# Two transformer blocks on one core: new prices in the clock that orders side work among weight products

## The chip, the cores and the metric

One core of a Trainium2 chip runs the whole program. The metric is the device time of one execution in microseconds; before the change the median of three runs is 2108.08 us (2105.86 to 2108.32).

## What is computed

The reference applies two layers of a first block and then two layers of a second block to a sequence of 256 tokens of width 1024, all in float32. A layer of the first block is a mixer (a gated linear recurrence, a forgetting attention of 8 heads with a cumulative decay, and a retention of 4 heads), a cross attention of 4 heads against a memory of 256 tokens, and a gated feed-forward of width 2816. A layer of the second block is a feed-forward, a mixer, and a feed-forward. Its mixer has a compressed, a selected and a window attention whose results are added under gates, a stick-breaking attention, and a window attention with sink logits:

```python
y_nsa = nsa_attention(...); y_sb = stick_breaking_attention(...); y_swa = swa_sink_attention(...)
merged = (g[:, :, 0] * (y_nsa @ w_up_nsa[l]) + g[:, :, 1] * (y_sb @ w_up_sb[l])
          + g[:, :, 2] * (y_swa @ w_up_swa[l]))
x = x + merged @ w_out[l]
```

## The kernel before

**Weight products.** All weights are read once, in pieces of 1 MB (raw). ScalarE rounds a piece to a high part (whi), VectorE subtracts to get the low part (wlo), and TensorE multiplies in three passes (high x high, high x low, low x high) in the dtype F32R. The activations, transposed, are held as thi and tlo; an output collects in a PSUM tile acc. A weight product of 512 columns is the unit of the main work. Weights.take and Weights.done (lines 235 to 265) hand out a piece and then start the splitting of the next. Callers are nat_blocks, stat_block, out_rows, fill_steps and, in the second mixer, up (line 1829).

**Side work.** What lies between the weight products (attention scores, softmax, transposes, normalisations) is written as generators. side(gen) (line 328) adds one to a list; pump() (line 336) advances those that are due. nat_blocks pumps after each half piece, which is six weight products of 512 columns; up pumps only in its second half. A generator yields the time at which its next step may come: True stands for the end of what it has just issued, None for at once, False for a flag to be waited for. Small products and transposes write to two PSUM banks called aux; two_aux() (line 370) waits until both are free. pairs() (line 375) is the pipeline of an attention over pairs of heads: scores, then row sums (rows), then transposes (turned), then value products (out), with waits between them. fox() (line 943) and nsa() (line 1665) use it, as do swa() and sb().

**The clock.** Nothing is measured while the program runs. The order is fixed when it is built, by the class Pace (line 49). It carries an estimated time for each engine, and nc.products is the time that TensorE has reached. Each call of an engine moves its time by a price: a fixed part and a part for each element (FIXED), a rate for TensorE, 360 GB/s and 1.5 us for a DMA. A step counts as due when its time is at most nc.products + 0.3, the advance. need(T, kt, t) (line 450) is asked before each weight product; if the k tile isn't made yet it pumps with force, which issues the earliest step whatever its time and moves nc.products there.

**What needs what.** In the first mixer the output products take k tiles 2 to 5 first; these are the forgetting attention's, which ends with value products into M. In the second mixer up(0, 4, 4, False) (line 1856) takes Y's k tiles 0 to 3, which nsa() writes in two groups of four units; a unit is one pair of heads in one branch, and the last group is tiles 2 and 3. Engines work through their own instructions in program order, so a step issued too early holds up what stands behind it on its engine.

Of the kernel before, what the change touches and what calls it, by code (L numbers as in the profile page):

```python
# [9 lines left out]
F32R = mybir.dt.float32r  # L10
# [38 lines left out]
class Pace:  # L49

    FIXED = {"vector": (0.065, 1.045e-3), "scalar": (0.075, 0.86e-3), "gpsimd": (0.13, 2.15e-3)}

    TABLES = {AF.Exp: ("exp", "ln"), AF.Tanh: ("exp",), AF.Ln: ("ln",), AF.Sin: ("sin",), AF.Sqrt: ("sqrt",), AF.Silu: ("silu",)}

    def __init__(self, nc):
        self.nc, self.table = nc, None
        self.products = self.end = 0.0
        self.at, self.written, self.read, self.free = {}, {}, {}, {}  # L60
        self.loads = 0.0
        for name in ("tensor", "vector", "scalar", "gpsimd", "sync"):
            self.at[name] = 0.0
            setattr(self, name, Paced(self, name, getattr(nc, name)))
# [22 lines left out]
    def op(self, name, op, args, kwargs):  # L87
# [15 lines left out]
        elif name == "tensor":  # L103
            moving = aps[2] if op == "matmul" else aps[0]
            rate = 1 if moving.dtype == F32R else 2 if op == "transpose" else 4
            self.products = start + max(0.027, size(moving) * rate / 2400.0) + 0.004
            done = self.products + 0.1
        else:
            fixed, each = self.FIXED[name]
            n = max(size(a) for a in aps)  # L110
            if kwargs.get("op") == ALU.pow:
                fixed, each = 0.3, 0.165
            if name == "scalar" and op == "activation":
                f = next((a for a in list(args) + list(kwargs.values()) if isinstance(a, AF)), None)
                if f in self.TABLES and self.table not in self.TABLES[f]:
                    self.table = self.TABLES[f][0]
                    self.at[name] = max(start, self.at[name]) + 1.3
            self.at[name] = max(start, self.at[name]) + (fixed + each * n) + (0.09 if kwargs.get("accum_out") is not None else 0.0)
            done = self.at[name] + 0.1
        for a in [out, kwargs.get("accum_out")]:  # L120
# [148 lines left out]
def tile_two_blocks(ctx, tc, I, out):  # L269
# [51 lines left out]

    def mm(ps, a, b, start, stop):
        nc.tensor.matmul(ps, a, b, start=start, stop=stop)

    def turn(ps, src, by):
# [10 lines left out]
    def pump(force=False):  # L336
# [15 lines left out]
        for _ in range(len(sides) + 1):  # L352
            ready = [i for i in sides if not i[2]]
            due = [i for i in ready if i[1] <= nc.products + 0.3 and aux_free() <= nc.products + 0.3]
            if due:
# [14 lines left out]
    def two_aux():  # L370

        while max([nc.idle(a) for a in auxs[-2:]], default=0.0) > nc.products + 0.3:
            yield max(nc.idle(a) for a in auxs[-2:])
# [30 lines left out]
    def pair_scores(q, k):  # L404

        pss = aux(), aux()
        for c, qs, ks in ((slice(0, P), slice(0, P), slice(0, P)), (slice(P, 384), slice(P, S), slice(0, S))):
            for u in (0, 1):
                mm(pss[u][:, c], q[HALF[u], qs], k[HALF[u], ks], start=True, stop=True)
        return pss  # L410

    def pair_scores_T(q, k):

        pss = aux(), aux()
        for c, ks, qs in ((slice(0, S), slice(0, P), slice(0, S)), (slice(S, 384), slice(P, S), slice(P, S))):
            for u in (0, 1):
                mm(pss[u][:, c], k[HALF[u], ks], q[HALF[u], qs], start=True, stop=True)
        return pss
# [19 lines left out]
    def pair_pv(dst, ws, vs, start=True, stop=True):  # L438

        for kt, (c0, c1, q0) in enumerate(((0, S, 0), (S, 384, P))):  # L440
            for u in (0, 1):
                mm(dst[HALF[u], q0:S], vs[u][:, kt, :], ws[u][:, c0:c1], start=start and kt == 0, stop=stop and kt == 1)

# [442 lines left out]
    def mixer1(l, T, cos, sin, next_maker):  # L886
        with nc.pool(tc, name=nm("mix1"), bufs=2) as mp:
# [26 lines left out]
            def forget(a):  # L914
# [24 lines left out]
                nc.vector.tensor_copy(c, ps[:8, :S])  # L939
                nc.sync.dma_start(cdram, c)  # L940


            def fox():
# [33 lines left out]
                def out_(b):  # L977
# [4 lines left out]
                    if b % 2 == 1:  # L982
                        put_T(M, 1 + b, ob[0])

                load_nb(0)
                load_nb(1)
# [1050 lines left out]
```

## Time and profile before

| | us |
|---|---|
| median of three runs | 2108.08 |
| the profiled execution | 2107.61 |
| its span, first to last instruction | 2105.8 |
| TensorE products busy | 2053.1 |
| VectorE busy | 1276.0 |
| ScalarE busy | 1120.7 |
| GpSimd busy | 84.7 |

The mean granted clock of TensorE is 0.995 of full speed. A line of the profile is always L150 in this kernel, because all calls pass through one helper there; instructions are told apart by their tiles (out<-in, buffer numbers left out). acc is a weight product; aux and o are side products. The end of a product is modelled and overlaps the next, so the distance between starts tells its cost better than its length. An fp32 product of the side work shows as two instructions, a transpose and an F32R product as one.

### The profile page before, as it was taken

To read this page: it belongs to the slowest core of one execution; us is meant where nothing else is said; L and a number is where in the kernel's file an instruction comes from. 1 tells how busy PE (TensorE), PEld (TensorE's weight loads), DVE (VectorE), ACT (ScalarE), POOL (GpSimd) and SP (SyncE) were. 2 spreads that over 40 slices of the span, in tenths; PEclk is the share of its full clock that TensorE was granted. 3 is DMA by queue.
4 is the path that set the end of the run, shared out by engine and by line. 5 is a ranking of instruction groups with operands and counts; after the bars stand their busy time and mean duration, and the time that the engine had idled before them with its cause. 6 is when DMAs were issued, how large, how long until landed. Compare 5 with 4: busy or idle time off the path is not lost.

```text
span 2105.8 us, 28507 instructions
## 1 busy us (share of the span) xinstructions
PE 2053.1 (97%) x10982; PEld 1717.3 (82%) x10982; DVE 1276.0 (61%) x2187; ACT 1120.7 (53%) x1910; POOL 84.7 (4%) x110
## 2 busy tenths in 40 slices
PE   7999999999899999999999999999999999999999
PEld 6889888888797788788888767888888887768887
DVE  6766566556664755655467666664655567756553
ACT  5556566455465654555355655554555456446552
POOL 0210000002100000000001000000000001000000
PEclk9999999999999999999999999999999999999999
DMA  7555565654465565555646544555555547545553
GB/s 244 182 194 190 186 212 180 212 178 158 148 225 175 182 198 191 172 187 180 210 145 207 169 140 158 193 176 193 180 196 194 162 151 230 144 132 183 179 197 103
DMA packets 204583, 380.86 MB, mean 181 GB/s; under 512 B 14160, under 2 KB 78464, under 8 KB 204448
## 3 DMA queue, kind: packets, MB, share of 16 engines
q1 hardware_dynamic: 192928, 366.46, 53.1%
q10 hardware_dynamic: 11520, 12.59, 2.0%
q8 instruction: 86, 1.41, 0.3%
q14 instruction: 49, 0.40, 0.1%
HBM read 372.03 MB, written 6.99 MB: 180 GB/s over the span
## 4 chain that ended last, share of the span: by engine, by line
PE 83%; DVE 6%; ACT 4%; DMA 4%; issue 2%; POOL 0%; SPq 0%; ACTq 0%; DVEq 0%; POOLq 0%
PE acc L150 74%; PE aux L150 6%; DVE wlo L150 3%; PE o L150 3%; ACT whi L150 1%; DMA nb<-cdram 1%; DMA raw<-in_w_in_dram 1%; DMA w<-in_nsa_cmp_k_w_dram 1%; ACT rn L150 1%; ACT thi L150 1%; DMA kvd<-kvout 0%; SPq L150 0%; DVE t L150 0%; DVE h L150 0%; DMA mem<-in_mem_dram 0%
## 5 line engine op out<-in xcount | busy, mean ns | idle before, releaser
L150 PE MATMUL acc<-whi,thi 128*128 128x512 f32 (+2 forms) x1856 | 716.2, 386 | 2.3 <-ACT thi L150 1.4
L150 PE MATMUL acc<-whi,tlo 128*128 128x512 f32 (+2 forms) x1856 | 699.9, 377 | 2.5 <-DVE tlo L150 2.4
L150 PE MATMUL acc<-wlo,thi 128*128 128x512 f32 (+2 forms) x1856 | 699.3, 377 | 3.1 <-DVE wlo L150 2.8
L150 DVE TENSOR_TENSOR wlo<-raw,whi 128x1024 fp32r<-128x1024 f32 (+1 forms) x386 | 463.0, 1210 | 310.1 <-ACT whi L150 308.3
L150 ACT CAST whi<-raw 128x1024 fp32r<-128x1024 f32 (+1 forms) x386 | 393.7, 1037 | 243.9 <-PE acc L150 219.9
L150 DVE SCALAR_TENSOR_TENSOR wlo<-raw,prm,whi 128x512 fp32r<-128x512 f32 (+1 forms) x640 | 398.5, 680 | 173.8 <-ACT whi L150 173.6
L150 ACT ACTIVATE whi<-raw,prm 128x512 fp32r<-128x512 f32 (+1 forms) x640 | 379.9, 663 | 90.2 <-PE acc L150 86.7
L150 PEld LDWEIGHTS acc<-whi,thi 128*128 128x128 f32 x1856 | 350.3, 189 | 72.4 <-issue 9.3
L150 PEld LDWEIGHTS acc<-whi,tlo 128*128 128x128 f32 x1856 | 349.9, 189 | 70.3 <-DVE tlo L150 6.4
L150 PEld LDWEIGHTS acc<-wlo,thi 128*128 128x128 f32 x1856 | 350.5, 189 | 64.4 <-DVE wlo L150 6.1
L150 PE MATMUL acc<-whi,ahi 128*128 128x512 f32 x528 | 206.9, 392 | 0.0
L150 PE MATMUL acc<-whi,alo 128*128 128x512 f32 x528 | 205.7, 389 | 0.0
L150 PE MATMUL acc<-wlo,ahi 128*128 128x512 f32 x528 | 205.6, 389 | 0.0
L150 PEld LDWEIGHTS acc<-whi,alo 128*128 128x128 f32 x528 | 99.1, 188 | 20.8
L150 PEld LDWEIGHTS acc<-whi,ahi 128*128 128x128 f32 x528 | 99.2, 188 | 19.9
L150 PEld LDWEIGHTS acc<-wlo,ahi 128*128 128x128 f32 x528 | 99.2, 188 | 19.9
L150 POOL TENSOR_TENSOR r<-v,mhalf 128x1 f32<-128x1 f32 (+3 forms) x46 | 48.1, 1047 | 1593.9 <-DVE v L150 1591.9
L150 PE MATMUL acc<-thi,whi 128*128 128x256 f32 x384 | 111.9, 291 | 0.0
L150 PE MATMUL acc<-tlo,whi 128*128 128x256 f32 x384 | 108.6, 283 | 0.0
L150 PE MATMUL acc<-thi,wlo 128*128 128x256 f32 x384 | 108.5, 283 | 0.0
L150 DVE SCALAR_TENSOR_TENSOR silu<-acc,r,silu 128x512 f32<-128x512 f32 (+1 forms) x72 | 47.5, 702 | 100.4 <-PE acc L150 100.4
L150 ACT CAST ahi<-aux 128x512 fp32r<-128x512 f32 (+1 forms) x72 | 39.8, 553 | 121.9 <-PE aux L150 121.7
(301 smaller groups left out, 1946.9 us busy)
## 6 DMA issues: line engine op xcount, KB each, us to landing
raw<-in_w_in_dram SPq DMA_DIRECT2D x65, 1024.0 KB, 5.1
raw<-in_ffn_w_gate_dram SPq DMA_DIRECT2D x44, 1024.0 KB, 5.1
raw<-in_ffn_w_up_dram SPq DMA_DIRECT2D x44, 1024.0 KB, 5.1
raw<-in_ffn_w_down_dram SPq DMA_DIRECT2D x44, 1024.0 KB, 4.9
raw<-in_w_gate_dram SPq DMA_DIRECT2D x22, 1024.0 KB, 5.0
raw<-in_w_up_dram SPq DMA_DIRECT2D x22, 1024.0 KB, 5.1
raw<-in_w_down_dram SPq DMA_DIRECT2D x22, 1024.0 KB, 4.8
raw<-in_w_out_dram SPq DMA_DIRECT2D x16, 1024.0 KB, 5.0
```

Source lines behind the costliest of these rows:

```text
L150: return f(*args, **kwargs)
```

## The change

Pace gets other prices. VectorE, ScalarE and GpSimd have larger fixed parts; activations have a price of their own; a sum that an activation collects costs 0.19 us more instead of 0.09; results count as ready 0.15 us after an engine's end (0.1 before) and 0.25 us after TensorE's (0.1 before). A transpose costs 0.109 us; the second product of a pair that runs on the other half of the array (beside) 0.007 us, where before it cost as much as the first; a weight product its columns and 32 more at 2.4 GHz; going from weight products to side products or back 0.09 us. The advance of 0.3 us is taken out of pump() and two_aux(). The prices of DMAs stay. In the first mixer forget() now sets a flag when it has issued the write of cdram, and fox() waits for that flag before its first loads. The arithmetic is the same in all steps.

```diff
-    FIXED = {"vector": (0.065, 1.045e-3), "scalar": (0.075, 0.86e-3), "gpsimd": (0.13, 2.15e-3)}
+    FIXED = {"vector": (0.15, 1.06e-3), "scalar": (0.14, 0.89e-3), "gpsimd": (0.25, 3.3e-3)}
...
-            rate = 1 if moving.dtype == F32R else 2 if op == "transpose" else 4
-            self.products = start + max(0.027, size(moving) * rate / 2400.0) + 0.004
-            done = self.products + 0.1
+            main = moving.dtype == F32R
+            if op == "transpose":
+                took = 0.109
+            elif self.beside:
+                took = 0.007
+            elif main:
+                took = (size(moving) + 32) / 2400.0
+            else:
+                took = max(0.224, size(moving) * 4 / 2400.0)
+            self.products = start + took + (0.09 if main != self.main else 0.0)
+            self.main = main
+            done = self.products + 0.25
...
-                fixed, each = 0.3, 0.165
+                fixed, each = 0.5, 0.22
...
-            self.at[name] = max(start, self.at[name]) + (fixed + each * n) + (0.09 if kwargs.get("accum_out") is not None else 0.0)
-            done = self.at[name] + 0.1
+            if name == "scalar" and op == "activation":
+                fixed, each = 0.3, 0.8e-3
+            self.at[name] = max(start, self.at[name]) + (fixed + each * n) + (0.19 if kwargs.get("accum_out") is not None else 0.0)
+            done = self.at[name] + 0.15
...
-    def mm(ps, a, b, start, stop):
+    def mm(ps, a, b, start, stop, beside=False):
+
+        nc.beside = beside
         nc.tensor.matmul(ps, a, b, start=start, stop=stop)
+        nc.beside = False
...
-            due = [i for i in ready if i[1] <= nc.products + 0.3 and aux_free() <= nc.products + 0.3]
+            due = [i for i in ready if i[1] <= nc.products and aux_free() <= nc.products]
...
-        while max([nc.idle(a) for a in auxs[-2:]], default=0.0) > nc.products + 0.3:
+        while max([nc.idle(a) for a in auxs[-2:]], default=0.0) > nc.products:
...
-                mm(pss[u][:, c], q[HALF[u], qs], k[HALF[u], ks], start=True, stop=True)
+                mm(pss[u][:, c], q[HALF[u], qs], k[HALF[u], ks], True, True, beside=u > 0)
...
                 nc.sync.dma_start(cdram, c)
+                flags.add("cdram")
...
+                while "cdram" not in flags:
+                    yield False
                 load_nb(0)
```

The same beside=u > 0 stands in pair_scores_T and pair_pv.

## Rows read from the trace of the kernel before

**Rows 1.** The page's table of engines: busy us, share of span, instructions.
```profile
PE 2053.1 (97%) x10982; PEld 1717.3 (82%) x10982; DVE 1276.0 (61%) x2187; ACT 1120.7 (53%) x1910; POOL 84.7 (4%) x110
```

**Rows 2.** Chain that ended last, a feed-forward stage: start us, length us, what.
```profile
328.31 20.45 PE acc L150 x90
```

**Rows 3.** Busy us by engine in a second mixer and a feed-forward; then clock, DMA.
```profile
1070.00:1280.00 210.00, 202.19 (x1156) 160.20 (x1156) 138.77 (x299) 115.09 (x218) 10.48 (x6) 0.99 0.54 166
...
1492.00:1682.00 190.00, 188.95 (x908) 158.02 (x907) 109.56 (x152) 97.34 (x149) 1.24 (x3) 1.00 0.56 187
```

**Rows 4.** TensorE's waits in the whole span: total us, times, longest us.
```profile
PE aux L150 <- DVE rn L150: 6.0, 4, 2.1
PE aux L150 <- DMA w<-in_nsa_cmp_k_w_dram: 3.8, 2, 2.6
PE aux L150 <- DVE rs L150: 2.9, 2, 1.5
...
PE aux L150 <- ACT cqT L150: 2.4, 2, 1.2
...
PE o L150 <- DVE rvg L150: 2.2, 1, 2.2
PE aux L150 <- DVE sc L150: 2.0, 1, 2.0
PE aux L150 <- DVE fT L150: 1.9, 1, 1.9
...
PE aux L150 <- DVE rot L150: 1.7, 2, 1.5
...
PE aux L150 <- ACT pt L150: 1.1, 1, 1.1
```

**Rows 5.** Chosen stretches, as rows 3 (the third last column is granted clock).
```profile
77.40:80.80 3.40, 3.40 (x11) 2.58 (x11) 3.29 (x8) 0.96 (x2) 0.00 (x0) 0.50 0.39 115
538.20:545.00 6.80, 6.61 (x30) 6.10 (x31) 3.50 (x10) 2.48 (x3) 0.87 (x2) 0.50 0.23 87
...
1253.90:1266.80 12.90, 9.09 (x49) 5.32 (x48) 5.03 (x21) 4.37 (x14) 0.00 (x0) 0.87 0.00 1
...
1869.60:1881.00 11.40, 7.87 (x49) 4.46 (x48) 5.00 (x21) 4.02 (x13) 0.00 (x0) 1.00 0.00 1
```

**Rows 6.** Timeline, short windows: start us, length us, engine, operation, [idle before, releaser].
```profile
1216.64 0.82 PE L150 MATMUL aux<-ident,rn 128*128 128x128 f32 x6
1217.21 0.49 PE L150 MATMUL acc<-whi,thi 128*128 128x512 f32 x1
1217.54 0.40 PE L150 MATMUL acc<-wlo,thi 128*128 128x512 f32 x1
...
1218.47 0.40 PE L150 MATMUL acc<-whi,tlo 128*128 128x512 f32 x1
1218.79 0.93 PE L150 MATMUL aux<-kT,qT 64*128 64x128 f32 x8
1219.65 0.50 PE L150 MATMUL acc<-whi,thi 128*128 128x512 f32 x1
...
1248.80 0.93 PE L150 MATMUL aux<-kT,qT 64*128 64x128 f32 x8
...
1250.15 0.40 ACT L150 ACTIVATE rn<-rn,nngm 128x128 f32<-128x128 f32 x1 [2.10 <-DVE nngm L150]
...
1251.83 0.18 ACT L150 ACTIVATION_READ_ACCUMULATOR rn<-rn,nngm 128x1 f32 x1
...
1255.79 1.16 PE L150 MATMUL aux<-ident,rn 128*128 128x128 f32 x6 [0.98 <-DVE rn L150]
...
1261.35 1.44 PE L150 MATMUL aux<-ident,rn 128*128 128x128 f32 x6 [2.06 <-DVE rn L150]
...
148.60 0.87 PE L150 MATMUL o<-pt,fv 128*64 128x256 f32 x8
149.40 0.50 PE L150 MATMUL acc<-whi,thi 128*128 128x512 f32 x1
```

More of the change, by code (lines that the diff above doesn't have):

```diff
@@ L61, in __init__ @@
         self.loads = 0.0
+        self.beside = False
+        self.main = True
         for name in ("tensor", "vector", "scalar", "gpsimd", "sync"):
@@ L416, in pair_scores_T @@
             for u in (0, 1):
-                mm(pss[u][:, c], k[HALF[u], ks], q[HALF[u], qs], start=True, stop=True)
+                mm(pss[u][:, c], k[HALF[u], ks], q[HALF[u], qs], True, True, beside=u > 0)
         return pss
@@ L441, in pair_pv @@
             for u in (0, 1):
-                mm(dst[HALF[u], q0:S], vs[u][:, kt, :], ws[u][:, c0:c1], start=start and kt == 0, stop=stop and kt == 1)
+                mm(dst[HALF[u], q0:S], vs[u][:, kt, :], ws[u][:, c0:c1], start and kt == 0, stop and kt == 1, beside=u > 0)
     def put_T(T, kt0, ob):
```

## The prediction

> **What bounds the kernel now.** I read the page's engine table first. TensorE multiplies for 97% of the span, VectorE works for 61% and ScalarE for 53% [rows 1]. The chain of waits shows what that busy time is. In its long pieces 90 weight products of 512 columns take 20.45 us, 0.227 us each, with nothing between them [rows 2]. Where only weight products run, the planner can win nothing. The table by stage shows where it is otherwise: in a second mixer TensorE is without work for 7.8 us of 210, in a feed-forward stage for 1.0 of 190 [rows 3]. The list of TensorE's waits names what it waits for. The start aside, it is tiles of side work of the mixers and the cross attention: rn, rs, cqT, rvg, sc, fT, rot, pt, and a small weight load by DMA [rows 4]. The table of chosen stretches adds the granted clock: 0.50, that is 1.2 GHz for 2.4, in two stretches of the first mixer, each during or right after such waits [rows 5].
>
> So two things can move. One is steps issued before their input is ready: TensorE, which works in program order, stands. The other is steps issued later than they could be: the chain of a mixer then isn't done when its result is needed, and TensorE stands at the end. The second is seen in both layers of the second mixer. There the weight products want Y's third k tile, the window and selection attention has not delivered it, and the planner forces what is left: 12.9 us in the first layer, 11.4 us in the second, with almost no weight product in it [rows 5].
>
> **The change part by part.** It changes no computation; it prices the same calls differently, so that pump() issues them at other places. The work on TensorE stays: only waits, visits and clock move. (A visit to side work costs about 0.19 us: the last weight product before one is followed after 0.32 us and the first after one after 0.33 us, where 0.23 is the rule [rows 6].)
>
> *Steps too early.* The old prices let the step after a pair of score products come 1.82 us after them: 0.10 for TensorE, 0.199 + 0.10 for the first VectorE pass, 1.32 for four exponentials with sums, 0.10 to finish; the advance takes 0.30 off, so 1.52 us. The trace has 2.35 us, from the end of the products at 1249.66 (1248.80 plus the 0.86 that the same group takes at 1218.79) to the last accumulator read at 1252.01 [rows 6]. So such a step is issued 0.8 us early, unless the grid of pump calls (six weight products, 1.36 us) rounds it up. That is the origin of waits on rs (2.9 us), cqT (2.4), sc (2.0) and fT (1.9), 9.2 us in all [rows 4]. New prices cover each: I count 8.0 us gone, bounds 3 and 9.2.
>
> *Waits that the new prices don't see.* rvg (2.2 us): the step asks for a flag that is set when the copy is issued, and no time is asked for, before or after. rot (1.7): VectorE stands for a DMA of decay rows, and the DMA lines are unchanged. pt (1.1): ScalarE stands behind an output copy. These 5.0 us go only where the steps land elsewhere: I count 2.0 us gone, bounds 0 and 5.0. The wait on the compression weights (3.8 us) is a DMA too: 0, bounds 0 and 3.8.
>
> *Clock.* The stretch 77.4 to 80.8 follows the wait on sc: 3.4 us at half rate cost 1.7. The one at 538.2 to 545.0 lies in the rvg and rot waits and costs up to 3.4 [rows 5]. I count the first and a third of the second: 2.8 us gone, bounds 0 and 5.1.
>
> *Steps later than needed.* A unit of the selection and window attention has three waits. Scores to row sums: 1.52 us before; now 0.25 + 0.286 + 0.15 + 2.57 + 0.15 = 3.41 us. Row sums to transposes: two small operations and four scalings, 1.30 - 0.30 before, 1.87 now; the value products between them used to push the planner's clock by 1.30 us and now do by 0.85, so 0.45 more is to be waited. Transposes to the next scores: 1.01 - 0.30 before, 1.36 now. Together 1.89 + 0.87 + 0.45 + 0.65 = 3.86 us more for each unit. In the trace three units take 30.0 us, from the scores at 1218.79 to those at 1248.80 (first and last of four) [rows 6]: 10.0 each, of which 2.8 us is TensorE's own (0.86 scores, 0.80 values, 0.57 transposes, three visits at 0.19; the 0.80 is that of the same eight products in the other mixer at 148.60) and the rest 5.3 grid steps. With the new waits rounded up to the grid, 3 to 4 + 1 to 2 + 1 to 2, it is 5 to 8 steps, 6.5 in the middle. So each unit is later by 2.0 us (by the rounding) to 3.9 us (by the sum). Three units: 6 to 12 us. The four units before them share their two banks with other chains whose prices rise as well; their delay can't be read from a row, and I put it between 2 and 12 us. At 12 to 14 us a unit the chain arrives at the forced place 0.6 to 2 units short; I take 1.5.
>
> What is a unit worth there? In the forced stretch two successive transposes stand at 1255.79 and 1261.35, 5.56 us apart [rows 6]. Of this, 2.8 us would have been paid earlier anyway. So a unit pushed into the tail costs 2.76 us: 1.5 x 2.76 x 2 layers = 8.3 us added, bounds 0 and 16.6 (three units).
>
> Here a rule of the Trainium skill speaks against the change. The four exponentials follow one another at 1250.15 and end with the last read at 1252.01: 1.86 us, so a read of 0.18 us overlaps the next exponential [rows 6]. The page "ScalarE: Activation LUTs" (Rules for kernel authors) has about 0.3 us for an ACTIVATE plus 0.83 ns an element; that is an estimate of 1.84 us for these four, and the trace agrees. By that rule the change's 2.57, which adds 0.19 for each sum, is 0.7 us too long, and the rows step would be held back by half a grid step without need.
>
> *The first mixer's end.* Its forgetting attention ends with the value products at 148.60; the output products start behind them at 149.40 [rows 6], and need this tile only in their third piece, two pieces of 12 products or 5.4 us later. The same added wait over four units is 8 to 15 us, so one step may be forced there. It would stand for little, since in the trace its inputs are ready long before: 1.0 us added over both layers, bounds 0 and 6. The new flag for cdram holds fox() until the row sums are written; with a flag already set it costs nothing, else one pump.
>
> *New places, new waits.* Every side step of the mixers may land on a busier moment of VectorE or ScalarE. I add 1.0 us, bounds -2 and 5. The feed-forward stages have few side steps and no wait to lose: 0.
>
> **The sum**, against the profiled execution's 2107.6 us (span 2105.8 and 1.8 around it): - 8.0 - 2.0 - 2.8 + 8.3 + 1.0 + 1.0 = - 2.5, so 2105.1. The median of the runs shown is 2108.1, 0.5 above that execution, so 2105.6; I say 2105.5.
>
> **The rivals.** *Gains without the loss.* The rounding eats the longer prices, the tails stay, and all early steps are cured: - 9.2 - 3 - 4 and nothing added, about 2092, and 2102 if only the sure part goes. For it: in the four units of the trace the steps already wait for the grid. Against it: 3.86 us is nearly three grid steps, too much to be rounded away three times in a row.
>
> *The tail takes over: slower.* One mechanism, in one place: the forced stretch before Y's third k tile in both layers of the second mixer. At three units late it costs 16.6 us, and with half of the savings (6.4) and the other additions (2.0) the time is 2108.1 + 16.6 - 6.4 + 2.0 = 2120; with 2.3 units 2116. It decides from where added tail exceeds the savings: 12.8 - 2.0 = 10.8 us, or about 2 units a layer. For it: 3.86 us a unit over eight units is 31 us, over two periods. Against it: five to six units lie in stretches where other chains hold them back already. The clock joins in: in the first layer's tail it was 0.87 on average, in the second's 1.00, with like gaps in the work [rows 5], so it can fall there but need not. The page "TensorE: Matmul & The Clock Gate" (What's actually happening) holds that idleness brings the engine to half rate; by that rule longer tails would run at 1.2 GHz in both layers and add, estimated from the 3.4 us stretch of these rows, up to 1.7 us each.
>
> *It does little.* The grid decides most steps, the order hardly changes, and the waits named above are DMA and queue waits that no engine price cures: 2106 to 2111.
>
> **How the numbers follow.** Chances: forecast (losses and gains nearly balance, 2100 to 2111) 0.38; gains without loss (2092 to 2102) 0.28; tail takes over (2111 to 2121) 0.25; little 0.09. About 0.2%, 4.2 us, is what a measurement of this kernel can tell from no change. Faster by more, below 2103.9: 0.13 of the forecast's and all 0.28 of the first rival, 0.41. Slower by more, above 2112.3: 0.23 of the tail's, 0.03 of the forecast's, 0.01 of the last: 0.27. The rest is 0.32. Cases of both signs hold most of the chance, so the range over all is 2094 to 2118 beside the forecast's own 2100 to 2111.
>
> **What would show it.** In the profile after: the waits on cqT, sc, fT and rs shrink to under 3 us together, while rvg, rot and the compression weights may stay. Full clock at 77 to 81 us. In the second mixer fewer units before the forced stretch: score products further apart than 10.0 us, and a stretch of 15 to 22 us in place of 12.9. I am wrong if that stretch is no longer than before, if the waits on these four tiles persist, or if the feed-forward stages change.

## The result, and the profile after

The changed kernel takes 2164.98 us, median of four runs (2162.41 to 2166.85), against 2108.2 us for the kernel before on the same chip: a ratio of 1.0265, 95% interval 1.0242 to 1.0287. It is slower by 57 us, where 2105.5 was predicted and 2118 was the upper end. The profiled execution has a span of 2160.6 us and a mean granted clock of 0.979 (2105.8 and 0.995 before).

The page's table of engines shows that no work was added: the same 10982 products, with TensorE counted busy for 24.5 us more and the span 54.8 us longer, so by this count 30.3 us of it are standing time and 24.5 us go to products that took longer [rows 1].

```profile
PE 2077.6 (96%) x10982; PEld 1736.8 (80%) x10982; DVE 1279.1 (59%) x2187; ACT 1125.7 (52%) x1912; POOL 81.2 (4%) x110
```

Where it is lost can be read without guessing, because both kernels issue the same 9312 weight products in the same order. The table subtracts the start of the same weight product in the two traces; it is worked out from these starts, a negative number means that the kernel named is ahead of the kernel before, and a difference between two columns is what the stretch between them cost. Product 456 is where the first mixer wants the memory's k tiles, 768 its third output piece; 5616 wants Y's sixth k tile, 5736 its zeroth, 5748 its third; the other layer's places follow in the right columns. (Sixth and zeroth are tiles 6 and 0, counted from 0; what the prediction calls the third is tile 2, written together with tile 3.)

```
us ahead (-) or behind (+) of the kernel before, at the same weight product
weight product                 444    480    840   1008   2784   2880   5100   5610   5640   5760   8200   8250   8400    end
changed kernel               -11.2   10.2   16.7   15.2   -3.2   12.2   11.9    4.8   21.0   34.2   23.4   39.4   54.7   54.8
advance 1.2 in the mixers     -5.9   -4.2    2.6    1.0  -12.5   -8.9   -9.3  -15.3   -7.3   -2.5   -9.7   -1.6    4.0    4.1
activation prices alone       -5.3   -4.0   -4.0   -5.5  -18.2  -15.7  -12.5  -14.6   -0.8   -1.4   -6.4    8.5    8.6    8.6
  the same, first block only  -4.0   -2.6   -2.8   -4.3  -17.2  -14.6  -11.5  -10.5  -10.4   -8.7  -11.0  -11.0  -11.0  -10.9
  and 0.6 in second mixers    -3.7   -2.3   -2.4   -4.0  -16.7  -14.1  -15.3  -16.3  -16.1  -18.9  -19.8  -18.3  -22.0  -22.0
before, 0.9 in 2nd mixers     -0.5   -0.5   -1.2   -1.2   -3.7   -3.7   -4.1   22.5   23.3    7.0   31.7   32.6   17.5   17.5
advance 2.0 everywhere         6.5    5.3    4.5    4.5   10.5   15.7   35.1   57.9   58.2   42.3   73.4   76.0   59.0   65.1
```

In the first row the changed kernel is 11.2 us ahead at product 444, loses 21.4 us by product 480, gains 18.4 us in the second layer's first mixer by product 2784 (15.2 to -3.2), loses 15.4 at its third piece, and loses 16.2 and 13.2 in the second mixer at the places where Y's tiles are wanted (4.8 to 21.0, then 21.0 to 34.2), and 16.0 and 15.3 in the other layer. Between these places it is mostly level or ahead. A part of what it is ahead is side work put off, which counts again at the next such place; so the fair sums are those over whole stages: 15 us lost in the first layer's first mixer, 3 gained in the second's, nothing in the cross attention and the feed-forward stages (12.2 to 11.9), and 22.3 and 20.5 lost in the two second mixers. How finely the table can be read shows in its fourth and fifth rows: up to product 5100 TensorE has the same order in these two kernels, and they stand 3.8 us apart there (-11.5 and -15.3).

The table of chosen stretches, read as [rows 5], shows these places: first the stretch that was at half clock before, then four forced ones.

```profile
77.40:80.80 3.40, 3.40 (x17) 2.82 (x16) 3.29 (x6) 3.24 (x7) 1.43 (x2) 1.00 0.24 62
90.20:107.10 16.90, 11.05 (x49) 8.71 (x47) 7.96 (x18) 3.34 (x7) 0.00 (x0) 0.64 0.34 108
1218.20:1233.20 15.00, 10.44 (x50) 7.70 (x50) 9.17 (x35) 4.03 (x14) 0.00 (x0) 0.66 0.21 76
1266.40:1272.90 6.50, 4.02 (x27) 2.55 (x25) 2.81 (x12) 5.05 (x13) 0.00 (x0) 1.00 0.36 129
1276.90:1301.10 24.20, 18.85 (x86) 11.57 (x84) 7.70 (x43) 9.98 (x34) 0.00 (x0) 0.65 0.07 23
```

The early clock loss is gone from its place (1.00 at 77 to 81 us). The forced stretch before Y's third k tile is 24.2 us where it was 12.9, and three of the four lie partly at half rate. Those before the memory's tiles and before Y's sixth and zeroth are not there in the kernel before.

TensorE's waits over the whole span (total us, times, longest) have changed owners [rows 4]. cqT, fT, rs, rvg and the compression weights have left the list. The largest that are there now belong to forced steps: sc and rot at the first mixers' forced places, kcb before Y's sixth tile, rn in the tails.

```profile
PE aux L163 <- DVE rn L163: 8.9, 6, 2.1
PE aux L163 <- DVE sc L163: 8.3, 2, 6.2
PE aux L163 <- DVE kcb L163: 7.0, 2, 3.5
...
PE aux L163 <- DVE rot L163: 4.4, 2, 3.7
```

Two timelines show one unit on its way. TensorE first: two successive score products of the window and selection attention stand 16.4 us apart (1239.79 and 1256.22), with 60 weight products between them besides the value products and the transposes.

```profile
1239.79 0.93 PE L163 MATMUL aux<-kT,qT 64*128 64x128 f32 x8
...
1246.32 0.87 PE L163 MATMUL o<-rn,vsw 128*64 128x256 f32 x8
...
1252.74 0.49 PE L163 MATMUL aux<-ident,rn 128*128 128x128 f32 x3
...
1256.22 0.93 PE L163 MATMUL aux<-kT,qT 64*128 64x128 f32 x8
```

Now VectorE and ScalarE in the same unit: the exponentials start at 1241.82, the last sum is read at 1243.69 (1243.50 plus 0.19), and the four scalings that the transposes need end at 1248.88.

```profile
1241.82 0.41 ACT L163 ACTIVATE rn<-rn,nngm 128x128 f32<-128x128 f32 x1 [1.81 <-DVE nngm L163]
...
1243.50 0.19 ACT L163 ACTIVATION_READ_ACCUMULATOR rn<-rn,nngm 128x1 f32 x1
...
1247.46 0.17 DVE L163 RECIPROCAL nsum<-nsum 128x4 f32<-128x4 f32 x1
...
1247.87 1.01 DVE L163 TENSOR_SCALAR rn<-rn,nsum 128x128 f32<-128x128 f32 x4
```

The transposes start 3.9 us after their input was ready. That alone doesn't make the changed kernel late. This is the third unit of eight, and the third unit of the kernel before waits as long: 17.2 us and 60 weight products from its scores to the next (1201.60 to 1218.79), and 3.9 us from the end of its scalings (1211.76 plus 1.01) to its transposes at 1216.64 [rows 6].

```profile
1157.90 0.93 PE L150 MATMUL aux<-kT,qT 64*128 64x128 f32 x8
...
1180.56 0.93 PE L150 MATMUL aux<-kT,qT 64*128 64x128 f32 x8
...
1201.60 0.93 PE L150 MATMUL aux<-kT,qT 64*128 64x128 f32 x8
...
1211.76 1.01 DVE L150 TENSOR_SCALAR rn<-rn,nsum 128x128 f32<-128x128 f32 x4
```

What is late is the place of the whole chain. The next table counts the weight products issued before a step of the second mixer, from the same two traces; in the other layer every number is higher by 2592.

```
weight products issued before the step              before   changed   later by
first transposes of the attentions (ta)               5118      5118          0
stick-breaking attention, first pair (rs,lneg)        5148      5160         12
stick-breaking attention, second pair                 5190      5220         30
attention with sinks, first scores (wkT,wqT)          5424      5466         42
window and selection, first scores (kT,qT)            5448      5496         48
attention with sinks, second scores                   5502      5586         84
window and selection, second scores                   5526      5616         90
window and selection, third scores                    5580      5640         60
window and selection, fourth scores                   5640      5700         60
```

The lateness grows from the start of the stage through all three attentions, to 90 weight products or 20.4 us at 0.227 us each; the forced stretch before Y's sixth tile takes 30 of them back. At Y's third tile four units still have their transposes to come, in the kernel before two.

### The profile page after: what moved, and what is told of

It is laid out like the page before. It is cut to its first block, busy times and chain, and to the rows that moved or that the text cites. A ratio compares the mean times of both kernels' runs of the same rounds, so it can differ in the third digit from the quotient of the medians.

```text
span 2160.6 us, 28554 instructions
## 1 busy us (share of the span) xinstructions
PE 2077.6 (96%) x10982; PEld 1736.8 (80%) x10982; DVE 1279.1 (59%) x2187; ACT 1125.7 (52%) x1912; POOL 81.2 (4%) x110
## 4 chain that ended last, share of the span: by engine, by line
PE 88%; DVE 6%; ACT 3%; DMA 1%; issue 1%; POOL 0%; SPq 0%; ACTq 0%; DVEq 0%; POOLq 0%
PE acc L163 77%; PE aux L163 8%; PE o L163 3%; DVE wlo L163 3%; ACT whi L163 1%; ACT rn L163 1%; DMA raw<-in_w_in_dram 1%; ACT thi L163 1%; DMA nb<-cdram 0%; DVE h L163 0%; DVE t L163 0%; DVE tlo L163 0%; DVE merged L163 0%; DVE x L163 0%; DVE rn L163 0%
## 5 line engine op out<-in xcount | busy, mean ns | idle before, releaser
L163 PEld LDWEIGHTS acc<-whi,thi 128*128 128x128 f32 x1856 | 349.6, 188 | 77.9 <-ACT thi L163 10.1
L163 PEld LDWEIGHTS acc<-whi,tlo 128*128 128x128 f32 x1856 | 349.2, 188 | 74.7 <-DVE tlo L163 11.5
L163 PEld LDWEIGHTS acc<-whi,alo 128*128 128x128 f32 x528 | 99.1, 188 | 20.7
```

The costliest lines, as they stand in the source:

```text
L163: return f(*args, **kwargs)
```

## The experiments

Theory A, throughout: a dearer estimate makes the waits of a chain longer; nothing is lost while weight products fill the time, but the chain is not done where its tile is wanted, and there the planner issues the rest with TensorE standing. All ratios are to the kernel before on the same chip, with 95% intervals. "Tail" is the forced stretch before Y's third k tile in the first and the second layer, from the first side product to the next weight product, read from the traces: 12.9 and 11.8 us in the kernel before, 24.2 and 24.1 in the changed one. (The 11.4 us of [rows 5] end at 1881.00; the next weight product comes at 1881.40.)

```profile
1869.65 0.87 PE L150 MATMUL o<-rn,vsw 128*64 128x256 f32 x8
...
1881.40 0.50 PE L150 MATMUL acc<-whi,thi 128*128 128x512 f32 x1 [0.68 <-ACT thi L150]
```

### Which part of the estimate does it

**The old engine prices put back into the changed kernel.**

```diff
-    FIXED = {"vector": (0.15, 1.06e-3), "scalar": (0.14, 0.89e-3), "gpsimd": (0.25, 3.3e-3)}
+    FIXED = {"vector": (0.065, 1.045e-3), "scalar": (0.075, 0.86e-3), "gpsimd": (0.13, 2.15e-3)}
...
-            if name == "scalar" and op == "activation":
-                fixed, each = 0.3, 0.8e-3
```

The price of a power, the 0.09 for a sum and the 0.1 of latency went back too.

> Theory A: the dearer VectorE, ScalarE and GpSimd prices and latencies make each step of a side chain fall due later, so the chains of three or four waits a unit are not done when the weight products want their tile, and the planner issues what is left at once, with TensorE standing. With the old engine prices back (TensorE's new prices, no advance and the flag kept) the chains are in time again: 2100 to 2120 us, no forced stretch before the memory's k tiles or before the first mixer's third piece, and some 13 to 16 us before Y's third k tile. Rival B: the planner's clock runs slower during side work, because pairs cost one and side products are cheap, or the advance is gone, and that is what makes the chains late; then 2145 to 2165 us, with the forced stretches of the changed kernel all still there.

Measured: 2128.91 us, ratio 1.0095 (1.0078 to 1.0111); tail 17.7 and 16.3 us, longer than expected, and 5.2 us before Y's sixth tile. Some 37 us of the loss are gone, and so are the forced stretches in the first mixers before the third piece and at the memory's tiles; 20 us stay, more than Theory A allowed for and less than Rival B wanted. TensorE's prices or the advance do something of their own.

**The new engine prices alone, in the kernel before** (with the flag for cdram). The dearer power, the 0.19 for a sum and the 0.15 of latency are in it too.

```diff
-    FIXED = {"vector": (0.065, 1.045e-3), "scalar": (0.075, 0.86e-3), "gpsimd": (0.13, 2.15e-3)}
+    FIXED = {"vector": (0.15, 1.06e-3), "scalar": (0.14, 0.89e-3), "gpsimd": (0.25, 3.3e-3)}
...
+            if name == "scalar" and op == "activation":
+                fixed, each = 0.3, 0.8e-3
```

> The kernel before with only the new engine prices and latencies (and the flag for cdram); TensorE's old prices and the advance of 0.3 stay. Theory A: nearly the whole loss, 2150 to 2175 us, forced stretches of 12 us and more before the memory's k tiles, at the third output piece of the first mixers and before Y's sixth and third k tiles. Rival B: little of it, 2100 to 2120 us.

Measured: 2168.76 us, ratio 1.0279 (1.0251 to 1.0306); tail 24.2 and 22.4 us, and 19.9 us before Y's sixth tile. These prices alone (and the flag) make the whole loss, with the old advance and the old prices of TensorE in place.

**TensorE's new prices alone.**

```diff
-            rate = 1 if moving.dtype == F32R else 2 if op == "transpose" else 4
...
+            elif self.beside:
+                took = 0.007
...
+            done = self.products + 0.25
```

> The kernel before with only TensorE's new prices (pairs as one, transposes, changes between kinds, 0.25 of latency). Of the changed kernel's loss of 56 us, putting the old engine prices back left 20: TensorE's prices, the lost advance, or both. Theory A: less time is counted for side work, so the planner's clock is behind and the steps of Y's chain fall due later; 2112 to 2124 us, a stretch of 14 to 17 us before Y's third k tile, the first mixers unchanged. Rival B2: the prices are right and do nothing, and the 20 us are the advance: 2104 to 2112 us.

Measured: 2130.95 us, ratio 1.0106 (1.0083 to 1.0129), above the range of either theory; tail 19.4 and 19.1 us. The first mixers, which I had expected unchanged, were 3.6 us behind at product 2880; another 7.7 us were lost by product 3240, in the second layer's cross attention.

**The advance alone taken away.**

```diff
-            due = [i for i in ready if i[1] <= nc.products + 0.3 and aux_free() <= nc.products + 0.3]
+            due = [i for i in ready if i[1] <= nc.products and aux_free() <= nc.products]
```

> The kernel before with the advance of 0.3 us taken away and nothing else. Theory A: each wait of a chain is 0.3 us longer or rounds up to one more pump call of 1.36 us now and then: 2112 to 2124 us, with the stretch before Y's third k tile at 14 to 17 us and TensorE's waits on early steps (rs, cqT, sc, fT) smaller by 3 to 6 us. Rival B2: 0.3 us is lost in the rounding: 2104 to 2112 us.

Measured: 2127.56 us, ratio 1.0093 (1.0073 to 1.0114); tail 21.9 and 21.8 us, both above Theory A's ranges. Three tenths of a microsecond at each wait make the tail 9 to 10 us longer. So all three parts push the same way, and they do not add: alone they cost 60 (2168.76 less 2109.21), 24 and 20 us (2130.95 and 2127.56 less 2107.38), together 57. A reading that would fit, but that no run shows by itself: once the chain misses its place, a further delay moves units from one side of it to the other.

**One price alone**, that of the activation and its sum.

```diff
+            if name == "scalar" and op == "activation":
+                fixed, each = 0.3, 0.8e-3
-            ... + (0.09 if kwargs.get("accum_out") is not None else 0.0)
+            ... + (0.19 if kwargs.get("accum_out") is not None else 0.0)
```

> The kernel before with only the activation's new price (0.3 us and 0.8 ns an element) and the dearer sum (0.19 for 0.09): four exponentials cost 1.24 us more by the estimate, of which 0.4 is the sums. Theory A: one dearer kind of step is enough to make Y's chains late: a part of the loss, 2118 to 2140 us, forced stretches before Y's sixth k tile (8 to 12 us, absent before) and third k tile (15 to 18 us), the first mixers within 4 us of before. Rival B3: the loss needs VectorE's and the latencies' prices: 2104 to 2114 us.

Measured: 2112.3 us, ratio 1.0026 (1.0015 to 1.0037). The time lies in Rival B3's range and under Theory A's, but the forced stretch of Theory A is there. The table above shows that this is no small effect but two large ones: ahead by 12.5 us when the second mixers begin (product 5100), then 13.8 and 14.9 us lost before Y's sixth tile (-14.6 to -0.8, -6.4 to 8.5), with a forced stretch of 14.6 and 14.9 us there. The first mixers did not stay within 4 us of the kernel before, as I had expected, but gained (-18.2 at product 2784).

### Is it lateness

**An advance of 2.0 us in the changed kernel, everywhere.**

```diff
-            due = [i for i in ready if i[1] <= nc.products and aux_free() <= nc.products]
+            due = [i for i in ready if i[1] <= nc.products + 2 and aux_free() <= nc.products + 2]
```

> The changed kernel, with every step allowed 2.0 us ahead of its estimate. Theory A: lateness is the cause, so the forced stretches are gone, and the time falls by 45 to 75 us, to 2090 to 2120 us, with waits of TensorE on sc, fT, cqT or pt back at 10 to 20 us in all, since steps now come ahead of their input. Rival C: the new estimate puts steps at bad places, late or not, and the advance only adds waits: above 2145 us.

Measured: 2173.73 us, ratio 1.0312 (1.0292 to 1.0333). The tail is gone, as expected, and yet the time is worse: the expectation failed, and the time is one that Rival C allows. The list of TensorE's waits says where much of it goes: steps now come ahead of their input, also in the feed-forward stages, which had no such wait in either kernel.

```profile
PE aux L163 <- DVE silu L163: 28.2, 35, 0.9
```

**The advance in the mixers only, 1.2 us.**

```diff
+        nc.advance = 1.2 if ph in ("mixer1", "mixer2") else 0.0
```

> The changed kernel with an advance of 1.2 us in the first and second mixers, and none elsewhere. An advance of 2.0 everywhere took the second mixers' forced stretches away but lost 28 us in the feed-forward stages, where steps then came ahead of their silu, and made TensorE wait in the mixers. Theory A (lateness at the forced places, with a price for each step that comes too early): the feed-forward stages as in the changed kernel, the stretches before the memory's tiles and at the first mixers' third piece gone, those before Y's third k tile 15 to 20 us, so 2100 to 2130 us. Rival C (the new estimate places steps badly at any advance): 2145 us or more.

Measured: 2111.75 us, ratio 1.0021 (1.0012 to 1.0031); tail 16.6 and 16.7 us. With the estimate of the changed kernel untouched, one number leaves 4.4 us of its 57 (2111.75 less 2107.38). The forced stretch at the memory's tiles is gone (-5.9 at product 444, -4.2 at 480). The stretch before Y's sixth tile is 7.1 and 6.9 us, and the second scores of the window and selection attention come at product 5514, where the changed kernel has 5616 and the kernel before 5526. Rival C falls.

**An advance of 0.9 for 0.3 in the second mixers of the kernel before.**

```diff
+        nc.advance = 0.9 if ph == "mixer2" else 0.3
```

> The kernel before with an advance of 0.9 us for 0.3 in the second mixers only: lateness turned the other way. Theory A: the planner forces nothing in Y's chain any more, the stretches before Y's third k tile (12.9 and 11.4 us in the kernel before) shrink to 3 to 8 us, and TensorE's early waits in these stages grow by 3 to 8 us: 2098 to 2110 us. Rival F: the chain runs at the pace of its own operations, so that steps issued earlier only move the wait from the end into the units: 2106 to 2116 us, with more waits on rn and pt.

Measured: 2130.44 us, ratio 1.0089 (1.0071 to 1.0108), slower than either theory said. The second scores come at product 5460, the tail is gone entirely, and 16 us with it (23.3 to 7.0 at products 5640 and 5760), but 27 us were lost before (-4.1 to 22.5). Rival F was right that the wait moves forward, though not where: the largest is on the compression weights, a load by DMA, whose price the change leaves alone. In TensorE's waits it grew to 10.0 us, and in a timeline of the first layer's compression it stands for 4.9 us, in a stretch whose clock is 0.76.

```profile
PE aux L151 <- DMA w<-in_nsa_cmp_k_w_dram: 10.0, 2, 5.1
```
```profile
1182.53 1.07 PE L151 MATMUL aux<-ident,rs 128*128 128x128 f32 x6
...
1189.93 0.60 PE L151 MATMUL aux<-w,hh 128*30 128x64 f32 x4 [4.94 <-DMA w<-in_nsa_cmp_k_w_dram]
```
```profile
1177.00:1195.00 18.00, 12.48 (x57) 9.16 (x58) 8.37 (x24) 5.08 (x12) 0.80 (x2) 0.76 0.60 145
```

So early costs as well as late, and the time has its minimum between. The wait on these weights is only a part of the 27 us; the other waits in that stretch are too many and too small to be told one by one.

### Whose steps are forced

**Only the chain that makes the missing tile is forced**, others if it is held by a flag.

```diff
-                i = min(ready, key=lambda i: i[1])
+                rank = lambda i: of.index(i[0].__name__) if i[0].__name__ in of else len(of)
+                i = min(ready, key=lambda i: (rank(i), i[1]))
```

> The changed kernel, but where a k tile is missing the planner forces the steps of the chain that makes this tile first, and others only if that chain is held by a flag. Rival D: what costs is that forcing takes the earliest step of any chain and so pulls retention's, compression's and selection's steps along (five of retention's before the memory's k tiles); then those stretches shrink by 5 to 10 us each at three places, 2135 to 2150 us. Theory A: the steps pulled along are wanted a few products later anyway, so what is saved at one place is paid at the next: 2155 to 2175 us.

Measured: 2173.56 us, ratio 1.0304 (1.0286 to 1.0322). At the same weight products it loses only 8.2 us at the memory's tiles (21.4 in the changed kernel) and 5.2 before Y's sixth (16.2), and pays at the next places: at the end of the first mixer it is 15.8 us behind, the changed kernel 15.2, and the stretch before Y's zeroth tile is 20.8 us for 6.5. Rival D falls: the steps that force pulled along were wanted soon, and what is saved at one place is paid at the next.

### The clock in the forced stretches

In the changed kernel 88.7 us lie in stretches at half rate, in the kernel before 20.4. The sums under the tables of these stretches:

```profile
sum 88.70, PE 75.51 PEld 54.41 DVE 37.42 ACT 27.10 POOL 7.71; mean PE 8.39 PEld 6.05 DVE 4.16 ACT 3.01 POOL 0.86
```
```profile
sum 20.40, PE 20.21 PEld 15.49 DVE 11.13 ACT 6.82 POOL 1.66; mean PE 4.04 PEld 3.10 DVE 2.23 ACT 1.36 POOL 0.33
```

At full rate TensorE's 75.5 and 20.2 us would be half as long, so the clock costs at most 27.6 us more than before, (75.5 - 20.2) / 2. How much of that is hidden behind VectorE and ScalarE, two runs asked by keeping TensorE busy where it would stand.

**Zero products for 80% of the reckoned standing time.**

```diff
+                if warm:
+                    for _ in range(int(0.8 * (max(i[1], aux_free()) - nc.products) / 0.2267)):
+                        nc.tensor.engine.matmul(warm[0], zero[0], warm[1], start=False, stop=False)
```

> The changed kernel, in the same order, but where the planner forces a step for a k tile of the mixers' natural-layout products whose accumulator is already begun, TensorE first adds products with a zero matrix (which change no result) for 80% of the time that the planner reckons it will stand: 28 and 34 of them in the first mixers, 60 before Y's third k tile in each second mixer, 0.23 us each. It asks what the half clock in those stretches costs. Theory H: the half clock (17.1 of the 24.2 us before Y's third k tile) is a cost of its own; with TensorE kept busy the clock stays at full rate, a unit of the forced tail takes 5.2 us and not the 6.3 us that it takes at half rate, and each of these two stretches falls from 24.2 to 18 to 21 us: 2150 to 2160 us. Rival G: the units are bound by VectorE's and ScalarE's passes, so the clock in there is worth little and the zero products stand in the way of side products: 2162 to 2178 us.

Measured: 2175.94 us, ratio 1.0302 (1.0284 to 1.0319), a time in Rival G's range; tail 25.5 us in both layers. The clock is 1.00 in the tail, but the run doesn't tell: the eleven zero products before the value products fill time in which TensorE would not have stood, and a unit takes 7.14 us (1287.13 to 1294.26).

```profile
1287.13 0.81 PE L163 MATMUL aux<-ident,rn 128*128 128x128 f32 x6
...
1289.43 2.83 PE L377 MATMUL acc<-whi,zero 128*128 128x512 f32 x11
1292.19 0.87 PE L163 MATMUL o<-rn,vsw 128*64 128x256 f32 x8
...
1294.26 0.82 PE L163 MATMUL aux<-ident,rn 128*128 128x128 f32 x6
```

**The same for 40%.** Only the factor is changed.

> As the run before, with zero products for 40% of the reckoned standing time: 13 and 16 in the first mixers, 25 before Y's third k tile in each second mixer. With 80% the clock stayed at full rate in that stretch, but TensorE had no idle time left and a unit took 7.1 us, more than without them. Theory H: with the zero products inside the idle time a unit takes 5.2 to 5.6 us at full rate, for 6.3 at half: each of the two stretches falls from 24.2 to 19 to 22 us, 2150 to 2161 us in all. Rival G: the units are bound by VectorE's and ScalarE's passes, and the clock in there is worth under 1 us a stretch: 2162 to 2170 us. If the clock still falls to half rate in that stretch, the run doesn't tell.

Measured: 2154.69 us, ratio 1.0219 (1.0203 to 1.0235), under the changed kernel's interval of 1.0242 to 1.0287, which was taken in other runs. The tail is 20.8 and 20.7 us, at a clock of 1.00, and a unit takes 5.58 us (1288.82 to 1294.40).

```profile
1283.60:1306.50 22.90, 22.06 (x118) 13.43 (x117) 8.35 (x43) 10.86 (x34) 0.00 (x0) 1.00 0.08 24
```
```profile
1288.82 1.16 PE L163 MATMUL aux<-ident,rn 128*128 128x128 f32 x6
...
1294.40 1.16 PE L163 MATMUL aux<-ident,rn 128*128 128x128 f32 x6
```

In the changed kernel the clock falls inside this tail: the score products take 1.30 us in the first unit and 2.34 in the second, and the distance from transposes to transposes goes from 5.23 to 6.34 us.

```profile
1276.92 0.82 PE L163 MATMUL aux<-ident,rn 128*128 128x128 f32 x6
1277.98 1.30 PE L163 MATMUL aux<-kT,qT 64*128 64x128 f32 x8 [0.24 <-ACT rn L163]
...
1282.15 1.41 PE L163 MATMUL aux<-ident,rn 128*128 128x128 f32 x6 [2.06 <-DVE rn L163]
1283.49 2.34 PE L163 MATMUL aux<-kT,qT 64*128 64x128 f32 x8
...
1288.49 1.59 PE L163 MATMUL aux<-ident,rn 128*128 128x128 f32 x6 [1.19 <-DVE rn L163]
```

Inside the tail Theory H's figures are met: 3.4 and 3.3 us, of a growth of 11.3 and 12.3. But the traced execution doesn't keep them. Its clock falls earlier, at half rate from 1272.9 to 1283.1. Part of that lies in the stretch before Y's zeroth tile, which gets no zero products and takes 8.8 us in both layers; in the changed kernel it takes 6.5 us at a clock of 1.00. No zero product of this mixer stands ahead of it, so they are not its cause. From product 5640 to 5760 this run loses 13.0 us to the kernel before, the changed kernel 13.2. So the trace shows a clock loss ahead of the tail in place of one in it.

```profile
1269.90:1278.70 8.80, 6.35 (x28) 3.77 (x26) 3.83 (x16) 5.16 (x13) 0.00 (x0) 0.67 0.23 83
1272.90:1283.10 10.20, 9.53 (x30) 6.25 (x29) 3.66 (x16) 2.45 (x9) 0.00 (x0) 0.50 0.00 1
```

That the half clock is a cost of its own shows in the five executions of this run, which have one order and different clocks. The traced one is the slowest, 2165.65 us at a mean clock of 0.982; the fastest took 2153.23 us at 0.990. The time at half rate is 2 x (1 - clock) of the span, so 77.9 and 43.0 us: 34.9 us more of it go with 12.4 us more time, 0.36 us for each. Two executions of the kernel before (2104.07 us at 0.998, 2112.04 us at 0.991) give 0.27 in the same way. An estimate from these: the changed kernel's 68.3 us more at half rate (88.7 less 20.4) cost 18 to 24 of its 57 us.

### A version that keeps the gain

**The activation's new price in the first six stages only**, in the kernel before.

```diff
+            if name == "scalar" and op == "activation" and self.first:
+                fixed, each, accum = 0.3, 0.8e-3, 0.19
...
+        nc.first = i < 6
```

> The kernel before with the activation's new price and the dearer sum in the first six stages only (mixer, cross attention and feed-forward of both layers), the old estimate after them. With that price throughout, the run before this one was 13 us ahead of the kernel before when the second mixers began and gave back 18 us before Y's sixth k tile in each layer. Theory A: the same price gains where it removes early steps and no tile is wanted too soon, and loses only at a forced place; so the 13 us stay: 2092 to 2099 us. Rival E: that gain is not kept (it comes back as waits at the next stage, or the order in the second mixers changes with it): 2103 to 2112 us.

Measured: 2094.6 us, ratio 0.9924 (0.9905 to 0.9944). The gain stays; Rival E falls. This beats both kernels: the dearer price pays where it is applied to the first block alone.

**And an advance of 0.6 in the second mixers.**

```diff
+        nc.advance = 0.6 if ph == "mixer2" else 0.3
```

> The activation's new price in the first six stages and an advance of 0.6 us in the second mixers. Theory A: the gain of the first (13 us) and a small one of the second (0 to 5 us) add up, since they lie in different stages: 2088 to 2098 us. Rival E or F: 2103 to 2114 us.

Measured: 2085.83 us, ratio 0.9887 (0.9868 to 0.9906); tail 9.8 and 8.4 us. Better than expected, and the best of all: 26 us under the kernel before of the same runs, 2111.89. In the two second mixers it gains 6.7 us by the table (-15.3 to -22.0), where an advance of 0.9 lost 21.6 (-4.1 to 17.5). So doubling the advance gains there and tripling it loses.

## Why the prediction was wrong

The two signs were right, the balance was not. I had set 12.8 us of savings against 10.3 us of losses. The savings can be had, at about that size: with the activation's price in the first block alone 11.5 us were kept (product 5100). The losses are several times what I set: 42.8 us in the second mixers by whole stages and 15 in the first layer's first mixer.

**Steps too early (8.0), waits not seen (2.0), clock (2.8).** Right in kind. cqT, fT, rs and rvg are gone, and 77 to 81 us is at full clock. The wait on the compression weights, counted as 0, went too. The new clock losses in the forced stretches outweigh the old ones; a price for them stood only in the rival, at up to 1.7 us a tail.

**The tail of the second mixer (8.3, bounds 0 and 16.6): the step that failed first.** That units would fall short of the third k tile came true, and nearly in the number: two more than before are left there, for 1.5. But the term was mis-sized: it took a small delay and charged it at one place, and by whole stages 42.8 us were lost.

The delay of the units ahead was put between 2 and 12 us; by the second scores it is 20.4 us. The units that I measured were the last and fastest: 10.0 us is the mean of the last three, and the first three take 22.7, 21.0 and 17.2 (1157.90, 1180.56, 1201.60, 1218.79). So scores further apart than 10.0 us, which I had named as a sign, say nothing here; the place of the step says it.

A unit in the tail was charged at 2.76 us, as if 2.8 of its 5.56 had been paid earlier anyway. Two more units made the tails 11.3 and 12.3 us longer, the whole 5.6 to 6.2 each. The kernel was indeed ahead before that (11.9 to 4.8 from product 5100 to 5610), but only until the next place where a tile was wanted.

I also priced the step from the row sums to the transposes alone, 1.00 us before and 1.87 now. The planner puts it behind all work that it believes queued on VectorE. By its own sum this step of the unit shown is ready 5.3 us after it was issued, 3.1 us of that for the queue, and 2.2 us where no weight products run beside it; in the kernel before it is ready after 3.7 us, 2.2 of that for the queue, and the advance takes 0.3 off. So the wait grew by 1.9 us where I had 0.87. In this unit the grid hides it: four pump calls, where I said one to two, in both kernels.

**Places left out of the sum.** The chain makes more than one tile, and each is wanted at a place of its own. Before Y's sixth tile I had nothing, and 16.2 and 16.0 us were lost there (products 5610 to 5640 and 8200 to 8250). Before the memory's tiles I had nothing, and 21.4 us went there, of which some is work put off. The kernel before has no stretch at these places to look at, but its slack can be counted in its trace: the last TensorE step that such a place waits for stands 54 weight products ahead of it at the memory's tiles, 78 at Y's sixth, 42 at its zeroth and 24 at the first mixer's third piece, so 12.3, 17.7, 9.5 and 5.4 us. The steps come later than that in the changed kernel: up to 90 weight products in the second mixer, and 102 to 192 for the forgetting attention's scores in the first layer's first mixer.

**The first mixer's end (1.0, bounds 0 and 6).** I argued that its inputs are ready long before. It lost 6.5 us in the first layer and 15.4 in the second, so the upper bound was wrong as well. The slack that I named, 5.4 us, was smaller than the added wait of 8 to 15 us that stood beside it; that was enough to see a stretch there.

**The rivals.** "The tail takes over" named the mechanism and one of its places, and stopped at 2121 for the same reason. That longer tails and a clock at half rate would join came true (0.65 in the first layer's tail). The Trainium skill's page "TensorE: Matmul & The Clock Gate" (What's actually happening) says that idleness brings the engine down; the trace agrees in that the six long stretches at half rate (6.8 us and more) all begin inside a forced stretch, and the tails filled with zero products ran at 1.00. The size that I had estimated beside it, 1.7 us a tail, was too small: a tail without the half rate was 3.3 us shorter.

**The sums of the activations.** The estimate drawn from "ScalarE: Activation LUTs" (Rules for kernel authors) of the Trainium skill said that the new price is 0.7 us too long for four exponentials. The changed kernel's trace agrees: four exponentials with sums take 1.87 us (1241.82 to 1243.69), where the price is 2.57. By itself this price gains in the first block and loses in the second; it is not its truth that decides, but where it is applied.

What stays open: how the 57 us split between standing and half rate more exactly than the estimate of 18 to 24 us and the upper bound of 27.6 us; which wait begins the lateness of the second mixers; why the first mixers gain so much with the activation's price alone; and what the flag for cdram does by itself, which wasn't tried.

## What to carry to other kernels

An estimate that orders side work is a schedule, not a description: larger prices move steps later, and a little more at each wait adds up along all chains of a stage. Later is free only while nothing waits at a fixed place, so list every place where a chain's result is wanted and count its slack there in the trace, in weight products; where the delay is larger, the rest is paid in standing, and in TensorE's clock on top. To see where a chain falls behind, compare the same step in the two kernels: a unit that looks slow may be as slow in both. Early costs as well, so the advance is measured stage by stage: 0.6 us in the second mixers gained here, 0.9 lost.

## What was not expected of the hardware

The granted clock falls inside a single forced tail, and in it the group of eight score products goes from 1.30 us (full rate) to 2.34 us, while the transposes of a unit go from 0.82 to 1.59; a chain of side products that seems bound by VectorE and ScalarE becomes 1.1 us longer a unit (5.23 to 6.34). By the estimate above, half rate costs less than half of the time spent in it: 0.27 to 0.36 us for each microsecond. And TensorE, kept busy with products that change nothing, pays for them: 25 zero products in a tail made it 3.3 us shorter, 60 made it 1.3 us longer than it was, and in the execution with 25 the clock fell ahead of the tail.
